# A macaron transformer block on one core: the head of the first feed-forward with a fixed order on four engines, and a last matrix whose sums begin as products

## The chip, the cores and the metric

One Trainium2 chip, of which the kernel uses one core. A core has a matrix engine (TensorE, PE in the profile), a vector engine (VectorE, DVE), a scalar engine (ScalarE, ACT), a general engine (GpSimd, POOL) and an engine that mostly issues transfers (SyncE, SP). Matrix products are accumulated in PSUM, eight banks of 512 fp32 columns; everything else lies in SBUF or DRAM. The metric is the device time of one execution in microseconds (us), the median of the runs.

## The reference

One block of a streaming encoder works on a stream `h` of 16 meta tokens and 1024 frames, 1040 tokens of width 1024, in fp32:

```python
h = h + 0.5 * swiglu(rmsnorm(h, ffn1_norm[l]), ffn1_w_gate[l], ffn1_w_up[l], ffn1_w_down[l])
u = rmsnorm(h, mix_norm[l])
...
h = h + mixed @ w_out[l]
h = h + 0.5 * swiglu(rmsnorm(h, ffn2_norm[l]), ffn2_w_gate[l], ffn2_w_up[l], ffn2_w_down[l])
return rmsnorm(h, final_norm)[:, N_META:]
```

`swiglu(x, g, u, d)` is `(silu(x @ g) * (x @ u)) @ d` with an inner width of 2816. In the middle stand sliding-window attention and gated linear attention; the change leaves them alone.

## The kernel before, in words

**Numbers in two parts.** Each fp32 operand of a product is cut into a high part of the type fp32r, rounded by a copy on ACT, and a low part, the difference, taken on DVE. A product is then three matmuls: high by high, high by low, low by high. Cuts of weights are `plain_cut` (L272 to L282: ACT cast L278, subtraction L279), cuts of operands are `halves` (L288: ACT L291, DVE L292).

**Feed-forward in blocks of seven products.** The inner width is 22 blocks of 128. The last two (f = 20, 21: "heads") and the first two are computed as plain products in the head of the kernel; the other 18 use one level of Strassen's method: two halves of the tokens (520 each in the first feed-forward) by two halves of the width, seven products in place of eight (`PRODUCTS`), with sums of operands (`token_sums`, lines L309 to L315) and of weights (`Group.sums`, L492). All big products are issued at L508.

**The head of the first feed-forward.** Tokens stand in four chunks q0 to q3 of 256 or 264 tokens (`CH`, L569). SP loads rows of x and the weights of the head blocks. `put(q, m)` transposes a tile of x on TensorE (L597, tile `xps`), scales it and cuts it. For q0 and q1 (`first_put`, L607 to L611) the token's root mean square is not known yet: products run on the unscaled operand and `empty` multiplies the result by the root afterwards (L682). For q2 and q3 (`second_put`) ACT copies the raw tile (L622, `xr`), DVE makes the scaled operand (L623, `ub`), ACT casts the high part (L624) and DVE subtracts for the low part (L625). `head_products` (matmuls L672 to L674, PSUM tiles `pg` and `pu`, one bank each) makes gate and up of one head block on one chunk and runs "hooks", other work put between its 16 groups of three matmuls. `head_out` (L689 to L692) is silu, product and cut of the result. Squares for the roots are `square_x`, the roots are `root` (a POOL copy L645 makes the tile to be turned), their spreading over partitions is `spread`. `rescale(m)` (L631 and `halves`) scales the operand of q0 and q1 in place once the roots are there.

The order of ACT and DVE in this head is written by hand (`manual_schedule`); that of TensorE, SP and POOL is left to a scheduler. The order of blocks is (f, q) = (0,q0), (1,q0), (0,q1) and so on; the pair (q, f) is the key of the table `hooks`. Then `more(0)` and `more(1)` make blocks 0 and 1 on the four chunks from q0 to q3, and `token_sums` prepares the operands of the big products, which begin at 138.55 us.

**The last matrix.** `down` runs 10 steps of 7 slots. A step is one half of a group of four inner blocks; a slot is one Strassen product on two output rows, 24 matmuls. All blocks of h (16 of 128 x 520, or 512 in the second feed-forward) are loaded from DRAM at its start (`load_h`, L405), and after each product `add_half` (L408, DVE) adds half of a PSUM tile to one of them. SP loads the operands `tm` (L414, from DRAM where the gate and up stage put them) and the weights `raw` (L426, four parts of 256 KB a step); later groups' `tm` go through ACT's queue. `pump` writes out ("keeps") what the gate and up stage left over: ACT cast L300, DVE subtraction L301, two writes L302 and L303 on SP, from four buffers (`ttile`). The weights of a step are summed on POOL (L492) and cut by `halves` two slots ahead of their use.

After it, the remaining head blocks are multiplied (L801), the sum is finished (L408) and the operand of the projection is made (L130, L131). The 16 meta tokens are gathered in a small tile, cut (L812, L813), and 16 copies of 128 x 16 on POOL (L815, L816) put the parts into the projection's operands; squares of h (L821) and their sums on DVE (L823) follow for the next norm. The projection's products are L97 to L99.

Of the kernel before, what the change touches and what calls it, by code (L numbers as in the profile page):

```python
# [8 lines left out]
F32 = mybir.dt.float32  # L9
# [26 lines left out]
def hybrid_kernel(  # L36
# [29 lines left out]
    def ttile(name, dt=F32, n=512):  # L66
        return tmp.tile([P, TW], dt, tag="t", name=name)[:, 0:n]
# [168 lines left out]
    class Seven:  # L236
# [162 lines left out]
            self.ending = True  # L399


        def load_h(self, ms, r, c):
            for m in ms:
                self.h[m + r][c] = self.block("h2")
                nc.sync.dma_start(out=self.h[m + r][c], in_=self.h_src[c, m + r])  # L405

        def add_half(self, hm, ps):
            nc.vector.scalar_tensor_tensor(hm, ps, 0.5, hm, op0=ALU.mult, op1=ALU.add)  # L408

# [18 lines left out]
            return Group(self, *raws)  # L428

        def down(self, h_src):  # L430
            self.h, self.h_src = [[None] * 2 for _ in range(KT)], h_src
# [12 lines left out]
            for step in range(2 * NG):  # L444
                kg, half = step // 2, step % 2
                if half == 0:
                    ts, nxt = nxt, {}
                last = step == 2 * NG - 1
                for i, (r, c) in enumerate(WHERE):
                    if i + AHEAD < 7:  # L450
# [5 lines left out]
                    if kg + 1 < NG:  # L456
                        self.load_t(kg + 1, nxt, 7 * half + i, nc.scalar)
                    w = made.pop(0)
                    pss = [group.product(i, w, ts, (j * P, 2 * P + j * P), j, step) for j in range(2)]
# [79 lines left out]
    def load_x(t, eng):  # L539
        eng.dma_start(out=xt[t], in_=x[t * P:(t + 1) * P, :])  # L540
# [75 lines left out]
    def second_put(q, m, ps):  # L616
        c, c0, n = CH[q]
        if c0 == 0:
            ub[1][m], B[1][m] = ffn1.block("ub"), ffn1.operand(False, "tb")
        raw = s_pool.tile([P, WB], F32, tag="s", name="xr")[:, 0:n]  # L620
        u, hi = ub[1][m][:, c0:c0 + n], B[1][m][:, c0:c0 + n]
        nc.scalar.copy(raw, ps)  # L622
        nc.vector.scalar_tensor_tensor(u, ps, vec[:, G1 + m:G1 + m + 1], racc[:, N1 + c0:N1 + c0 + n], op0=ALU.mult, op1=ALU.mult)  # L623
# [60 lines left out]
    def head_out(f, q, pss=None):  # L684
        c, c0, n = CH[q]
        x, a = kept[f, c], ttile("a")[:, 0:n]
        hi, lo = x[:, c0:c0 + n], x[:, N1 + c0:N1 + c0 + n]
        g, u = pss or (hi.bitcast(F32), lo.bitcast(F32))
        nc.scalar.activation(a, g, AF.Silu)  # L689
        nc.vector.tensor_mul(a, u, a)  # L690
        nc.scalar.copy(hi, a)
        nc.vector.tensor_sub(lo, a, hi.bitcast(F32))  # L692
        if c0:
            nc.sync.dma_start(out=ffn1.last_dram[f, c], in_=x.bitcast(F32))

    with tc.manual_schedule(engines={nc.scalar.engine, nc.vector.engine}):
        turn_g1()
        square_x(0)  # L700
        square_x(1, eng=nc.vector)
        heads, done = [[], []], {}
        cuts = []
        for i in range(2):
            w, parts = ffn1.plain_cut(head_raws[i], nc.gpsimd if i else None, False)
            heads[0].append(w)
            cuts.append(parts)

        def cut(f, i, eng=None):
            heads[f].append(ffn1.plain_cut(head_raws[2 * f + i], eng))  # L710

        def put(q, m):
            (first_put if q < 2 else second_put)(q, m, turn_x(q, m))

        def do(fn, *a, **k):
            return lambda: fn(*a, **k)

        def emptied(f, q):
            return lambda: empty(f, q, done.pop((f, q)))

        def out_of(f, q):
            return lambda: head_out(f, q, done.pop((f, q), None))

        for m in range(KT):
            put(0, m)
            if m in (0, 3):
                cuts[0][m // 3]()
                cuts[1][m // 3]()
        v = nc.vector
        hooks = {  # L730
            (0, 0): {0: [do(root, 0)], 2: [do(cut, 1, 0, nc.gpsimd)], 6: [do(spread, 0), do(cut, 1, 1)],
                     9: [do(put, 1, 0)], 12: [do(put, 1, 1)], 14: [do(put, 1, 2)]},
            (0, 1): {0: [do(put, 1, 3)], 2: [do(put, 1, 4)], 4: [do(put, 1, 5)], 6: [do(put, 1, 6)], 8: [do(put, 1, 7)],
                     9: [do(square_x, 2, eng=v), do(square_x, 8, NM)], 11: [emptied(0, 0)], 12: [do(square_x, 3, eng=v)]},
            (1, 0): {0: [do(root, 1)], 1: [emptied(1, 0), do(square_x, 6)], 3: [do(square_x, 4, eng=v)], 5: [do(square_x, 7)],
                     6: [do(square_x, 5, eng=v)], 9: [do(spread, 1)], 11: [do(root, 2), do(root, 3)]},
            (1, 1): {0: [emptied(0, 1)], 3: [do(spread, 2), do(spread, 3)],
                     **{5 + m: [do(put, 2, m)] for m in range(KT)}},
            (2, 0): {2: [emptied(1, 1), out_of(0, 0)], **{4 + m: [do(put, 3, m)] for m in range(KT)}, 12: [out_of(1, 0)]},
            (2, 1): {0: [out_of(0, 1)], 2: [out_of(1, 1)], 4: [out_of(0, 2)],  # L740
                     **{5 + m: [do(rescale, m)] for m in range(KT)}},
            (3, 0): {4: [out_of(1, 2)]},
            (3, 1): {2: [out_of(0, 3)]},
        }
        for q in range(4):
            for f in range(LAST):
                done[f, q] = head_products(q, heads[f], hooks[q, f], f == 0)
# [20 lines left out]

    more(0)
    out_of(1, 3)()  # L770
    more(1)
    ffn1.token_sums(ub, between)
    turn_rest()
# [38 lines left out]
    nc.scalar.copy(mh, mt)  # L812
    nc.vector.tensor_sub(ml, mt, mh.bitcast(F32))  # L813
    for m in range(KT):
        nc.gpsimd.tensor_copy(n2.hi[m][:, S:T], mh[:, m, :])  # L815
        nc.gpsimd.tensor_copy(n2.lo[m][:, S:T], ml[:, m, :])  # L816
    for m in range(KT):
        for c in range(2):
            a = sums1[:, c * N1:(c + 1) * N1]
# [772 lines left out]
```

## Time and profile before

| what | value |
|---|---|
| time, median of 3 runs | 2083.16 us (2080.94 to 2083.75) |
| the profiled execution, its own time | 2081.6 us |
| its span, first to last instruction | 2079.9 us |
| mean granted clock of TensorE | 0.988 |
| TensorE busy | 2035.0 us (98%) |
| VectorE, ScalarE, GpSimd busy | 1354.7 (65%), 817.3 (39%), 205.2 us (10%) |

The profiled execution is one of its own, 1.56 us under the median; 1.7 us of it lie outside the span. Times inside the kernel are counted from the span's start. "L508" is line 508 of the kernel. In the lists, `out<-in` names the tiles an instruction writes and reads; the engine after "<-" is what ended the wait. The granted clock is the share of full speed at which TensorE's clock ran.

### The profile page before, as it was taken

To read this page: it belongs to the slowest core of one execution; us is meant where nothing else is said; L and a number is where in the kernel's file an instruction comes from. 1 tells how busy PE (TensorE), PEld (TensorE's weight loads), DVE (VectorE), ACT (ScalarE), POOL (GpSimd) and SP (SyncE) were. 2 spreads that over 40 slices of the span, in tenths; PEclk is the share of its full clock that TensorE was granted. 3 is DMA by queue.
4 is the path that set the end of the run, shared out by engine and by line. 5 is a ranking of instruction groups with operands and counts; after the bars stand their busy time and mean duration, and the time that the engine had idled before them with its cause. 6 is when DMAs were issued, how large, how long until landed. Compare 5 with 4: busy or idle time off the path is not lost.

```text
span 2079.9 us, 31770 instructions
## 1 busy us (share of the span) xinstructions
PE 2035.0 (98%) x12177; PEld 1805.6 (87%) x12177; DVE 1354.7 (65%) x2303; ACT 817.3 (39%) x1551; POOL 205.2 (10%) x240
## 2 busy tenths in 40 slices
PE   8899999999799999999999999999999999999998
PEld 7799999999799988888897778888888888878888
DVE  5866677667577775775345335567876767758775
ACT  5534444443222254664324222344444544422222
POOL 1000000001222171000100000120000000014212
PEclk9899999999999999999999999999999999999999
DMA  6324344349976131125311225641543543599722
GB/s 200 108 84 150 119 156 170 124 144 353 341 246 240 56 99 50 62 61 155 112 41 58 70 66 158 217 143 51 170 165 131 171 154 131 203 378 351 263 81 82
DMA packets 271657, 317.73 MB, mean 153 GB/s; under 512 B 23943, under 2 KB 187905, under 8 KB 271505
## 3 DMA queue, kind: packets, MB, share of 16 engines
q1 hardware_dynamic: 253856, 254.30, 37.2%
q10 hardware_dynamic: 17296, 61.29, 7.8%
q8 instruction: 96, 1.57, 0.3%
q14 instruction: 57, 0.46, 0.1%
q0 software_dynamic: 352, 0.11, 0.1%
HBM read 208.01 MB, written 107.63 MB: 152 GB/s over the span
## 4 chain that ended last, share of the span: by engine, by line
PE 90%; DMA 4%; DVE 3%; ACT 1%; issue 1%; POOL 1%; SPq 0%; DVEq 0%; POOLq 0%; ACTq 0%
PE pb L508 30%; PE pd L508 15%; PE pa L508 8%; PE pj L97 6%; PE pj L98 6%; PE pj L99 6%; PE br L97 1%; PE br L99 1%; PE br L98 1%; PE wo L97 1%; PE wo L98 1%; PE wo L99 1%; PE pd L801 1%; DMA tm<-f2mid 1%; PE tp L1057 1%; DMA h<-h_dram 1%
## 5 line engine op out<-in xcount | busy, mean ns | idle before, releaser
L508 PE MATMUL pb<-tt,wop 128*128 128x260 f32 (+1 forms) x2016 | 337.2, 321 | 0.0
L508 PEld LDWEIGHTS pb<-tt,wop 128*128 128x128 f32 x2016 | 294.5, 188 | 28.1
L508 PE MATMUL pb<-tm,wop 128*128 128x260 f32 (+1 forms) x1440 | 240.8, 323 | 15.9 <-DVE h L408 9.5
L291 ACT CAST wop<-s 128x512 fp32r<-128x512 f32 x232 | 143.7, 622 | 263.7 <-PE pb L508 90.5
L508 PEld LDWEIGHTS pb<-tm,wop 128*128 128x128 f32 x1440 | 211.6, 192 | 37.5 <-DVE h L408 8.7
L97 PE MATMUL pj<-u2h,whi 128*128 128x512 f32 (+2 forms) x608 | 230.3, 379 | 3.1 <-DVE o L1311 1.7
L98 PE MATMUL pj<-u2l,whi 128*128 128x512 f32 (+2 forms) x608 | 225.1, 370 | 3.3 <-POOL u2l L816 3.3
L99 PE MATMUL pj<-u2h,wlo 128*128 128x512 f32 (+2 forms) x608 | 225.2, 370 | 0.0
L292 DVE TENSOR_TENSOR wop<-s,wop 128x512 fp32r<-128x512 f32 x232 | 167.6, 724 | 86.4 <-ACT wop L291 85.9
L291 ACT CAST wop<-raw 128x512 fp32r<-128x512 f32 x174 | 108.3, 623 | 237.9 <-PE pb L508 112.5
L408 DVE SCALAR_TENSOR_TENSOR h<-pb,h 128x520 f32<-128x520 f32 (+1 forms) x160 | 110.4, 694 | 62.0 <-PE pb L508 59.5
L492 POOL TENSOR_TENSOR s<-raw 128x512 f32<-128x512 f32 x28 | 38.7, 1383 | 1087.5 <-DMA raw<-in_ffn_w_down 498.1
L97 PEld LDWEIGHTS pj<-u2h,whi 128*128 128x128 f32 x608 | 115.3, 190 | 22.6 <-issue 2.2
L98 PEld LDWEIGHTS pj<-u2l,whi 128*128 128x128 f32 x608 | 115.4, 190 | 18.7 <-POOL u2l L816 3.5
L99 PEld LDWEIGHTS pj<-u2h,wlo 128*128 128x128 f32 x608 | 115.1, 189 | 17.2
L292 DVE TENSOR_TENSOR wop<-raw,wop 128x512 fp32r<-128x512 f32 x174 | 122.1, 703 | 6.7 <-ACT wop L291 6.5
L508 PE MATMUL pd<-tm,wop 128*128 128x260 f32 (+1 forms) x720 | 118.9, 318 | 1.9 <-DVE h L408 1.8
L508 PEld LDWEIGHTS pd<-tm,wop 128*128 128x128 f32 x720 | 103.8, 188 | 12.0 <-DVE h L408 1.5
L192 ACT CAST whi<-raw 128x1024 fp32r<-128x1024 f32 x58 | 60.8, 1048 | 134.5 <-PE pj L98 77.5
L508 PE MATMUL pb<-tb,wop 128*128 128x260 f32 (+1 forms) x672 | 112.4, 321 | 1.1 <-DVE m L762 1.1
L508 PE MATMUL pa<-tb,wop 128*128 128x260 f32 (+1 forms) x672 | 112.3, 320 | 0.0
L508 PE MATMUL pd<-tb,wop 128*128 128x260 f32 (+1 forms) x672 | 112.3, 320 | 0.0
(379 smaller groups left out, 3771.5 us busy)
## 6 DMA issues: line engine op xcount, KB each, us to landing
tm<-f1mid ACTq DMA_DIRECT2D x56, 520.0 KB, 5.9
tm<-f2mid ACTq DMA_DIRECT2D x56, 512.0 KB, 5.9
raw<-in_ffn_w_gate SPq DMA_DIRECT2D x43, 512.0 KB, 3.9
raw<-in_ffn_w_up SPq DMA_DIRECT2D x43, 512.0 KB, 4.0
raw<-in_ffn_w_down SPq DMA_DIRECT2D x80, 256.0 KB, 6.2
f1mid<-kh SPq DMA_DIRECT2D x70, 260.0 KB, 2.8
f1mid<-kl SPq DMA_DIRECT2D x70, 260.0 KB, 2.7
f2mid<-kh SPq DMA_DIRECT2D x70, 256.0 KB, 2.9
```

The lines of the kernel that those rows point to most:

```text
L97: nc.tensor.matmul(ps, wh[k], xh[k], start=(k == 0), stop=False)
L98: nc.tensor.matmul(ps, wh[k], xl[k], start=False, stop=False)
L99: nc.tensor.matmul(ps, wl[k], xh[k], start=False, stop=(k == n - 1))
L192: nc.scalar.copy(hi[:, 0:cols], raw[:, 0:cols])
L291: nc.scalar.copy(x[:, 0:n], src)
L292: nc.vector.tensor_sub(x[:, n:2 * n], src, x[:, 0:n].bitcast(F32))
L408: nc.vector.scalar_tensor_tensor(hm, ps, 0.5, hm, op0=ALU.mult, op1=ALU.add)
L492: (eng.tensor_add if add else eng.tensor_sub)(a[s], a[x], a[y])
L508: nc.tensor.matmul(ps, y, x[:, c0 + s0:c0 + s0 + sn], start=(first and k == 0 and at == 0), stop=(at == 2 and k == len(cols) - 1), skip_gr ...
L801: nc.tensor.matmul(ps, y, x[:, c0 + s0:c0 + s0 + sn], start=(n == 0), stop=(n == 3 * LAST - 1), skip_group_check=True)
L1057: nc.tensor.transpose(ps[0:k, ga * P:(ga + 1) * P], s.p[:, ga, off:off + k], ident)
```

## The change

It has four parts.

1. **Head.** SP and TensorE get a written order as well (`manual_schedule` over four engines). The weights of the first head block come in four parts of four k-tiles, mixed with the loads of x. All sixteen transposes of q0 stand ahead on TensorE. Squares, roots, cuts and puts sit at other hooks; POOL's cut of a second head weight has no POOL copy ahead of it, the first head block's low parts are all subtracted on DVE, and the puts of q2 come three hooks later. The last subtraction of `second_put` and the second half of `head_out` are returned as a function and run behind the next put or output (`later`).
2. **Order of chunks.** `more` goes through q2, q3, q0, q1.
3. **Last matrix** (both feed-forwards). No h is loaded at the start. The first product of each of the 16 blocks is written as half of the PSUM tile by ACT. The old h comes later: two blocks a step in steps 1 to 8, through a `ttile` buffer, and DVE adds each a step after its load. Operands of the next group are loaded four slots later, and `pump` runs at slots 0, 1, 2, 4, 5, 7 and 8.
4. **Small copies.** The 16 copies of the meta tokens go from POOL to ACT.

On TensorE, at the start of `more(0)`; names with buffer numbers, `tb_185` an operand of q0 after its rescale, `tb_577` and `tb_591` operands of q2. Before:

```order
L672 MATMUL pg_1013<-tb_185,whi_1003 128x256
L672 MATMUL pu_1014<-tb_185,whi_1009 128x256
L673 MATMUL pg_1013<-tb_185,whi_1003 128x256
L674 MATMUL pg_1013<-tb_185,wlo_1004 128x256
L673 MATMUL pu_1014<-tb_185,whi_1009 128x256
L674 MATMUL pu_1014<-tb_185,wlo_1010 128x256
```
After:

```order
L690 MATMUL pg_1015<-tb_577,whi_1005 128x256
L691 MATMUL pg_1015<-tb_577,whi_1005 128x256
L692 MATMUL pg_1015<-tb_577,wlo_1006 128x256
L690 MATMUL pg_1015<-tb_591,whi_1005 128x256
L691 MATMUL pg_1015<-tb_591,whi_1005 128x256
L692 MATMUL pg_1015<-tb_591,wlo_1006 128x256
```
The chunk that stands first is q2, whose operands are made by the puts, where it was q0.

On DVE, the last two rescales and the first output that follows (of head block 1 on q2, the 128x256 product). Before:

```order
L631 SCALAR_TENSOR_TENSOR ub<-ub,vec,racc 128x520
L311 TENSOR_TENSOR ub<-ub 128x520
L309 TENSOR_TENSOR ub<-ub 128x520
L292 TENSOR_TENSOR tb<-ub,tb 128x520
L631 SCALAR_TENSOR_TENSOR ub<-ub,vec,racc 128x520
L310 TENSOR_TENSOR ub<-ub 128x520
L315 TENSOR_TENSOR ub<-ub 128x520
L292 TENSOR_TENSOR tb<-ub,tb 128x520
L690 TENSOR_TENSOR a<-pu,a 128x256
```
After (L649 is `rescale`, L708 and L712 are `head_out`):

```order
L649 SCALAR_TENSOR_TENSOR ub<-ub,vec,racc 128x520
L311 TENSOR_TENSOR ub<-ub 128x520
L309 TENSOR_TENSOR ub<-ub 128x520
L292 TENSOR_TENSOR tb<-ub,tb 128x520
L649 SCALAR_TENSOR_TENSOR ub<-ub,vec,racc 128x520
L310 TENSOR_TENSOR ub<-ub 128x520
L309 TENSOR_TENSOR ub<-ub 128x520
L292 TENSOR_TENSOR tb<-ub,tb 128x520
L708 TENSOR_TENSOR a<-pu,a 128x256
```
The product of the output still stands behind the eighth rescale; only the pairing of the token sums (L309 to L315) differs.

On SP, at the start of the first feed-forward's last matrix (`h` blocks loaded, `tm` operands, kept pairs `kh` and `kl`, `raw` weights). Before:

```order
L405 DMA h_5920<-x_dram 128x520
L414 DMA tm<-f1mid 128x1040 x2
L302 DMA f1mid<-kh 128x520
L303 DMA f1mid<-kl 128x520
L405 DMA h_5980<-x_dram 128x520
L405 DMA h_5982<-x_dram 128x520
L302 DMA f1mid<-kh 128x520
L303 DMA f1mid<-kl 128x520
L405 DMA h_6024<-x_dram 128x520
L405 DMA h_6026<-x_dram 128x520
L426 DMA raw_6233<-in_ffn_w_down 128x2x256 x2
L426 DMA raw_6236<-in_ffn_w_down 128x2x256
```
After:

```order
L409 DMA tm<-f1mid 128x1040 x10
L302 DMA f1mid<-kh 128x520
L303 DMA f1mid<-kl 128x520
L302 DMA f1mid<-kh 128x520
L303 DMA f1mid<-kl 128x520
L421 DMA raw_6191<-in_ffn_w_down 128x2x256 x2
L421 DMA raw_6194<-in_ffn_w_down 128x2x256 x2
L302 DMA f1mid<-kh 128x520
L303 DMA f1mid<-kl 128x520
L302 DMA f1mid<-kh 128x520
```
The loads of h are gone from between the operands and the kept pairs, and the third step's weights (`raw`, L421) stand behind the second kept pair, where the last part of them stood behind the seventh.

The diff, cut to its core:

```diff
-            nxt, AHEAD = {}, 2
+            AHEAD, LATE = 2, 4
...
-                self.load_t(0, nxt, at, nc.sync)
-                if at == 1:
-                    self.load_h((0, 1), 0, 0)
+                self.load_t(0, ts[0], at, nc.sync)
...
-                if at in (5, 7, 11):
-                    self.load_h((0, 1), *{5: (0, 1), 7: (4, 1), 11: (4, 0)}[at])
...
-                        self.add_half(self.by_parts(self.h[2 * half + j + r][c]), pss[j])
-                    self.pump()
-                    if step == 0 and i < 4:
-                        self.load_h((2, 3), *((0, 0), (0, 1), (4, 1), (4, 0))[i])
+                        m = 2 * half + j + r
+                        if self.h[m][c] is None:
+                            self.h[m][c] = self.block("h2")
+                            nc.scalar.activation(self.by_parts(self.h[m][c]), pss[j], AF.Copy, scale=0.5)
+                        else:
+                            self.add_half(self.by_parts(self.h[m][c]), pss[j])
+                    if slot in (0, 1, 2, 4, 5, 7, 8):
+                        self.pump()
+                    if step and i in (1, 4):
+                        if step > 1:
+                            m, c, x = coming.pop(0)
+                            nc.vector.tensor_add(self.h[m][c], self.h[m][c], x)
+                        if old and not last:
+                            m, c = old.pop(0)
+                            x = ttile("old", n=self.n)
+                            nc.sync.dma_start(out=x, in_=h_src[c, m])
+                            coming.append((m, c, x))
...
+    head_raw(0, 0)
     load_x(1, nc.sync)
-    head_raws = [ffn1.plain_raw(cols_view(w, HEADS[0] * P)) for w in (ffn1_w_gate, ffn1_w_up)]
+    for i, k in ((1, 0), (0, 4), (1, 4)):
+        head_raw(i, k)
...
-        nc.vector.tensor_sub(B[1][m][:, N1 + c0:N1 + c0 + n], u, hi.bitcast(F32))
         nc.sync.dma_start(out=x_dram[1, m, :, c0:c0 + n], in_=raw)
+        return lambda: nc.vector.tensor_sub(B[1][m][:, N1 + c0:N1 + c0 + n], u, hi.bitcast(F32))
...
-            (0, 0): {0: [do(root, 0)], 2: [do(cut, 1, 0, nc.gpsimd)], 6: [do(spread, 0), do(cut, 1, 1)],
-                     9: [do(put, 1, 0)], 12: [do(put, 1, 1)], 14: [do(put, 1, 2)]},
+        (0, 0): {6: [cut(1, 0, nc.gpsimd)], 8: [do(square_x, 1, eng=v)], 10: [cut(1, 1)], 12: [put(1, 0)], 14: [put(1, 1)]},
...
-                     **{5 + m: [do(put, 2, m)] for m in range(KT)}},
+                 **{8 + m: [put(2, m)] for m in range(KT)}},
...
-                     **{5 + m: [do(rescale, m)] for m in range(KT)}},
-            (3, 0): {4: [out_of(1, 2)]},
-            (3, 1): {2: [out_of(0, 3)]},
+                 **{8 + m: [do(rescale, m)] for m in range(KT)}},
+        (3, 0): {4: [out_of(1, 2)], 5: [later]},
+        (3, 1): {4: [out_of(0, 3)], 5: [later]},
...
-        for q, (c, c0, n) in enumerate(CH):
+        for q in (2, 3, 0, 1):
+            c, c0, n = CH[q]
...
-        nc.gpsimd.tensor_copy(n2.hi[m][:, S:T], mh[:, m, :])
-        nc.gpsimd.tensor_copy(n2.lo[m][:, S:T], ml[:, m, :])
+        nc.scalar.copy(n2.hi[m][:, S:T], mh[:, m, :])
+        nc.scalar.copy(n2.lo[m][:, S:T], ml[:, m, :])
```

More of the change, by code (lines that the diff above doesn't have):

```diff
@@ L399, in gate_ups @@
             self.ending = True
[L402 to L405, printed above, removed]
         def add_half(self, hm, ps):
@@ L430, in down @@
         def down(self, h_src):
[L431 to L432 removed]
+            self.h = [[None] * 2 for _ in range(KT)]
+            AHEAD, LATE = 2, 4
+            ts, old, coming = [{} for _ in range(NG)], [(m, c) for m in range(KT) for c in range(2)], []
             group = self.load_weights(0)
             for at in range(14):
[L435 to L437 removed]
+                self.load_t(0, ts[0], at, nc.sync)
                 if at == 3:
                     follow = self.load_weights(1)
[L440 to L441 removed]
             group.sums(nc.vector)
@@ L444, in down @@
             for step in range(2 * NG):
-                kg, half = step // 2, step % 2
-                if half == 0:
-                    ts, nxt = nxt, {}
+                half = step % 2
                 last = step == 2 * NG - 1
                 for i, (r, c) in enumerate(WHERE):
+                    slot = 7 * step + i
                     if i + AHEAD < 7:
@@ L455, in down @@
                         made.append(follow.weights(i + AHEAD - 7))
-                    if kg + 1 < NG:
-                        self.load_t(kg + 1, nxt, 7 * half + i, nc.scalar)
+                    kg, at = 1 + (slot - LATE) // 14, (slot - LATE) % 14
+                    if 0 < kg < NG:
+                        self.load_t(kg, ts[kg], at, nc.scalar)
                     w = made.pop(0)
-                    pss = [group.product(i, w, ts, (j * P, 2 * P + j * P), j, step) for j in range(2)]
+                    pss = [group.product(i, w, ts[step // 2], (j * P, 2 * P + j * P), j, step) for j in range(2)]
                     for j in range(2):
-                        self.add_half(self.by_parts(self.h[2 * half + j + r][c]), pss[j])
-                    self.pump()
-                    if step == 0 and i < 4:
-                        self.load_h((2, 3), *((0, 0), (0, 1), (4, 1), (4, 0))[i])
+                        m = 2 * half + j + r
[15 more added lines that the diff above has]
+                            coming.append((m, c, x))
                 if not last:
@@ new lines, in rest, with cut @@
+        def rest():
+            nc.scalar.copy(hi, a)
+            nc.vector.tensor_sub(lo, a, hi.bitcast(F32))
+            if c0:
+                nc.sync.dma_start(out=ffn1.last_dram[f, c], in_=x.bitcast(F32))
+        return rest
+    turn_g1()
+    square_x(0)
+    heads, done, behind = [[], []], {}, []
+    v = nc.vector
+    cuts = []
+    for i in range(2):
+        w, parts = ffn1.plain_cut(head_raws[i], None, False)
+        heads[0].append(w)
+        cuts.append(parts)
+    def cut(f, i, eng=None):
+        return lambda: heads[f].append(ffn1.plain_cut(head_raws[2 * f + i], eng))
@@ new lines, in later, with put, go, do @@
+    def later():
+        while behind:
+            behind.pop(0)()
+    def put(q, m):
+        def go():
+            ps = turn_x(q, m)
+            if q < 2:
+                first_put(q, m, ps)
+            else:
+                rest = second_put(q, m, ps)
+                later()
+                behind.append(rest)
+        return go
+    def do(fn, *a, **k):
+        return lambda: fn(*a, **k)
+    def emptied(f, q):
+        return lambda: empty(f, q, done.pop((f, q)))
+    def out_of(f, q):
+        def go():
+            rest = head_out(f, q, done.pop((f, q), None))
+            later()
+            behind.append(rest)
+        return go
@@ new lines, in hybrid_kernel @@
+    turned = [turn_x(0, m) for m in range(KT)]
+    for m in range(KT):
+        first_put(0, m, turned[m])
+        if m in (0, 3):
+            cuts[0][m // 3]()
+            cuts[1][m // 3]()
+    hooks = {
+        (0, 0): {6: [cut(1, 0, nc.gpsimd)], 8: [do(square_x, 1, eng=v)], 10: [cut(1, 1)], 12: [put(1, 0)], 14: [put(1, 1)]},
+        (0, 1): {0: [do(root, 0), put(1, 2)], 2: [put(1, 3)], 4: [put(1, 4)], 6: [put(1, 5)], 8: [put(1, 6)], 10: [put(1, 7)],
+                 12: [do(spread, 0)], 13: [do(square_x, 8, NM), do(square_x, 2, eng=v)]},
+        (1, 0): {0: [emptied(0, 0)], 1: [do(square_x, 6)], 2: [do(square_x, 3, eng=v)], 4: [emptied(1, 0)],
+                 5: [do(square_x, 7)], 6: [do(square_x, 4, eng=v)], 9: [do(root, 1)], 10: [do(square_x, 5, eng=v)],
+                 13: [do(root, 2), do(root, 3)]},
+        (1, 1): {0: [do(spread, 1)], 1: [emptied(0, 1)], 7: [do(spread, 2), do(spread, 3)],
+                 **{8 + m: [put(2, m)] for m in range(KT)}},
+        (2, 0): {2: [emptied(1, 1)], 3: [out_of(0, 0)], **{4 + m: [put(3, m)] for m in range(KT)}, 13: [out_of(1, 0)]},
+        (2, 1): {0: [out_of(0, 1)], 2: [out_of(1, 1)], 4: [out_of(0, 2)], 6: [later],
+                 **{8 + m: [do(rescale, m)] for m in range(KT)}},
+        (3, 0): {4: [out_of(1, 2)], 5: [later]},
+        (3, 1): {4: [out_of(0, 3)], 5: [later]},
+    }
@@ L748, in hybrid_kernel @@
+    for q in range(4):
+        for f in range(LAST):
+            done[f, q] = head_products(q, heads[f], hooks[q, f], f == 0)
+    manual.__exit__(None, None, None)
     ffn1.tops.update(B11=B[0][0:4], B21=B[0][4:8], B12=B[1][0:4], B22=B[1][4:8])
@@ L770, in hybrid_kernel @@
     out_of(1, 3)()
+    later()
     more(1)
```

51 lines of the change are left out of this document (8 added, 43 removed).

## The prediction, made before the result

> **What bounds the kernel now.** I read the page first, then the list of what TensorE waited for, then the chain of waits in the stretches that list points to, then busy time by stretch. The page says whose time it is:
>
> ```profile
> PE 2035.0 (98%) x12177; PEld 1805.6 (87%) x12177; DVE 1354.7 (65%) x2303; ACT 817.3 (39%) x1551; POOL 205.2 (10%) x240
> ```
>
> TensorE is the bound, so an edit can only give back time that TensorE loses, idle or at a low granted clock. The waits over the whole span (waiting matmul and line, what it waited for, us in total, times, longest):
>
> ```profile
> PE pb L508 <- DVE h L408: 9.5, 2, 8.5
> PE pb L508 <- DMA tm<-f2mid: 4.6, 4, 2.6
> PE pg L673 <- DVE tb L292: 2.9, 6, 0.8
> PE pj L98 <- POOL u2l L816: 3.3, 1, 3.3
> ...
> PE pb L508 <- DMA tm<-f1mid: 1.8, 2, 1.5
> ...
> PE pj L97 <- DVE h L408: 1.2, 1, 1.2
> ```
>
> The stretches they lie in, each row with its length, the busy time and count of each engine, the granted clock (PEclk), the DMA share and rate:
>
> ```profile
> 0.00:24.00 24.00, 17.29 (x83) 13.91 (x83) 7.87 (x20) 10.56 (x23) 6.84 (x16) 0.86 1.00 302
> ...
> 76.00:100.00 24.00, 18.75 (x85) 15.11 (x84) 23.14 (x38) 10.60 (x21) 0.00 (x0) 0.64 0.27 80
> 100.00:139.00 39.00, 37.88 (x317) 37.66 (x316) 19.40 (x36) 13.26 (x28) 0.00 (x0) 1.00 0.10 36
> ...
> 518.00:532.00 14.00, 12.18 (x87) 11.79 (x86) 8.35 (x13) 2.30 (x4) 0.00 (x0) 0.88 1.03 392
> 532.00:549.00 17.00, 14.10 (x114) 13.53 (x113) 8.77 (x14) 3.44 (x6) 0.00 (x0) 1.00 1.02 369
> 549.00:563.00 14.00, 5.53 (x34) 5.33 (x33) 7.47 (x9) 2.99 (x5) 10.77 (x8) 0.76 0.82 270
> ...
> 740.00:764.00 24.00, 19.39 (x121) 18.65 (x120) 16.06 (x31) 10.20 (x17) 18.55 (x42) 0.93 0.36 89
> ...
> 1852.00:1868.00 16.00, 12.09 (x41) 9.12 (x40) 4.82 (x8) 1.86 (x3) 0.00 (x0) 0.79 1.02 390
> 1868.00:1900.00 32.00, 32.00 (x142) 26.47 (x142) 25.05 (x38) 7.37 (x12) 12.67 (x9) 1.00 1.01 363
> ```
>
> At full clock a matmul of about 260 columns takes 37.88/317 = 0.1195 us (row 100 to 139), one of 512 takes 32.00/142 = 0.225 us (row 1868 to 1900). Length less count times that is what a stretch loses: 0 to 24 us 24 - 83 x 0.1195 = 14; 76 to 100 us 13.8 (its clock of 0.64 alone is 8.6 of it); 518 to 563 us 3.6 + 3.4 + 9.9 = 16.9; 1852 to 1868 us 16 - 41 x 0.225 = 6.8. In 740 to 764 us, where shapes are mixed, idle time 24 - 19.39 = 4.6 and clock 24 x 0.07 = 1.7 make 6.3. That is 58 us within the change's reach.
>
> **The head, to 139 us.** A "quarter" is the 48 matmuls of one f-block on one of the four token chunks q0 to q3, 48 x 0.1195 = 5.74 us. Rows of the chain before 100 us (start, length, what), then two timeline rows:
>
> ```profile
> 43.37 0.50 DVE ub L623
> ...
> 44.76 0.41 DVE ub L623
> ...
> 59.53 0.39 PE pg L672
> ...
> 75.32 4.77 DMA raw<-in_ffn_w_up
> ...
> 81.25 1.23 DVE wlo L279
> ...
> 88.09 0.67 DVE ub L631
> 88.76 0.61 DVE ub L311
> ...
> 89.98 0.61 DVE tb L292
> ...
> 93.80 0.63 ACT tb L291
> ```
>
> ```profile
> 23.68 2.37 POOL L279 TENSOR_TENSOR wlo<-rawx,whi 128x1024 fp32r<-128x1024 f32 x1
> ```
>
> ```profile
> 73.40 0.76 DVE L631 SCALAR_TENSOR_TENSOR ub<-ub,vec,racc 128x520 f32<-128x520 f32 x1
> ```
>
> Start: the second head block cannot begin before POOL's cut ends, 23.68 + 2.37 = 26.05. The change puts that cut ahead of the spreading copies and makes the transposes first, so the first quarter is paced by the put copies alone. I take the cut's end 3.6 us earlier, and give 0.6 back because the puts of q2 stand three hooks later in the next block (3 x 3 x 0.1195 = 1.1 at most): 3 us, between 0 (POOL's cut slower beside a busier DVE) and 5. The weights in parts move the same bytes; their first product starts a little earlier, inside that range.
>
> POOL's price may move. In 740 to 764 us eight small copies beside DVE's adds of two inputs took 9.76 us, eight after them 1.16:
>
> ```profile
> 746.47 9.76 POOL L815 CAST u2h<-mth 128x16 fp32r<-128x16 f32 x8 [1.88 <-ACT mth L812]
> ...
> 756.27 1.16 POOL L816 CAST u2l<-mtl 128x16 fp32r<-128x16 f32 x8
> ```
>
> [...] A cut of 5 us in place of 2.37 would cost the start about its whole gain, which is the range's 0.
>
> The delayed subtraction of the second puts (43.37 to 44.76: 1.3 us a put) I cost at nothing either way. Today a put is DVE product, ACT cast, DVE subtraction. Afterwards the next product still waits for ACT's next raw copy, which stands behind the cast on ACT: same length.
>
> The rescales: DVE begins them at 73.40 now. They come 3 us earlier with the rest, 1.2 because a weight cut (81.25: 1.23) goes behind the first of them, and by estimate 2.5 because the outputs (L690, L692) overlap in pairs: 66.7.
>
> The new chunk order: before, q0 runs first and each of its products follows its rescale. Afterwards q2 and q3, which need none. The second quarters (2,1), (3,0), (3,1) run from 59.53 to 59.53 + 3 x 5.74 = 76.8 now, 73.8 afterwards, and q2 ends at 79.5. But q3 needs two of the eight PSUM banks, and all eight are taken: the pair that comes free is that of (1,2), emptied by its silu on ACT, which stands behind the eighth rescale's cast. DVE's rows to there: 8 x 0.67 rescales, 7 x 0.61 subtractions L292, 7 x 0.61 token sums, 4 x 1.23 cuts make 18.8, and about 0.9 waiting for the second weights (4.77 us from issue to landing): 66.7 + 19.7 = 86.4. ACT's 0.63 cast and the silu, 0.4 by estimate, end at 87.4. So the waits of q0 go, and q3 waits 87.4 - 79.5 = 8 us instead. After such a stall the clock is half for a few us: 549 to 563 us has 0.76, 14 x 0.24 = 3.4 us of it partly under the stall; I take 1.9. Then seven quarters as now from 98 us, where the chain of rescales ends, to 138.55: 40.5. The big products start at 87.4 + 1.9 + 40.5 = 129.8, not 138.55: **8.7 us**, from 4 (start term 0) to 14 (rescales earlier still).
>
> **The last matrix of the first feed-forward, 500 to 563 us.** The chain there:
>
> ```profile
> 508.13 12.88 DMA tm<-f1mid
> ...
> 542.42 9.42 DMA raw<-in_ffn_w_down
> ...
> 552.03 1.23 POOL s L492
> ...
> 554.63 0.63 ACT wop L291
> ...
> 558.70 2.97 PE pb L508 x12
> ```
>
> A transfer takes 12.88 us with DMA share 1.03: the queue is full. The 16 loads of h are 260 KB each (16 x 0.266 = 4.3 MB, 10.9 us at 392 GB/s). They stand on SP among the tm loads and then among the kept tiles' writes, so the third step's last weights leave only at 542.42 and land at 551.84; POOL's sums, ACT's cast and a DVE operation ahead of L408 follow, and TensorE waits 8.5. Afterwards no h is loaded there; those weights stand after the second kept pair, and pumps are spread over slots 0 to 8. The weights then leave before 524 us by the order, 18 us earlier, and 9.42 later is still before need. What is late next is ACT, which waits in order for a buffer of the kept tiles at slots 6 to 8: 1 to 2 us and perhaps a clock step. The trace shows that a short wait can cost that: 518 to 532 us waited 1.8 us in all, and its clock is 0.88, 14 x 0.12 = 1.7 us.
>
> [...]
>
> Costs added, by rows of the page and of the groups of ACT:
>
> ```profile
> L408 DVE SCALAR_TENSOR_TENSOR h<-pb,h 128x520 f32<-128x520 f32 (+1 forms) x160 | 110.4, 694 | 62.0 <-PE pb L508 59.5
> ```
>
> ```profile
> L379 ACT COPY u<-pd 128x520 f32<-128x520 f32 x18 | 10.7, 595 | 23.7 <-PE pd L508 23.7
> ```
>
> Sixteen ACT copies (16 x 0.6 = 9.5 us) replace sixteen DVE additions in steps 0 and 1; sixteen DVE additions of about 0.69 us come in steps 2 to 9, two in each of 20 us, with DVE 65% busy: under TensorE, nothing. Without that cover they would cost 11 us. The next tm loads leave four slots later:
>
> ```profile
> tm<-f1mid ACTq DMA_DIRECT2D x56, 520.0 KB, 5.9
> ```
>
> The last then has 3 slots of 24 matmuls (3 x 2.87 = 8.6 us) against 5.9 us to land, so it stays hidden by 2.7 us. I leave 2.9 of 16.9: **14 us**, from 7 to 16.9.
>
> **The sixteen small copies after it.** They go from POOL to ACT; ACT's nearest row:
>
> ```profile
> 763.04 0.40 ACT L146 ACTIVATE u2t<-tot,eps_t 128x8 f32<-128x8 f32 x2 [11.07 <-PE tot L137]
> ```
>
> 16 x 0.2 = 3.2 us from 746.5 end before 750, where POOL's first eight now last to 746.47 + 9.76 = 756.2. The 3.3 and 0.2 waits and the 1.7 of clock go; the squares behind the copies on ACT shift by 3.2 but DVE's sums of them have until the totals. The 1.2 wait for L408 stays. 6.3 - 1.2 - 0.4 = **4.7 us**, from 3 to 5.2.
>
> **The second feed-forward's last matrix.** Its chain before the loss:
>
> ```profile
> 1832.02 9.20 DMA h<-h_dram
> ...
> 1847.84 12.39 DMA tm<-f2mid
> ```
>
> The first eight h loads (8 x 0.262 MB at 390 GB/s = 5.4 us) leave the queue ahead of that tm, which is up to 6 us late. Of 6.8 I take **6 us**, from 3 to 6.8.
>
> **Sum.** 8.7 + 14 + 4.7 + 6 = 33.4. The profiled execution was 2081.6 us (span 2079.9 and 1.7 around it), 1.56 under the median of 2083.16: 2081.6 - 33.4 = 2048.2, as a median 2049.8.
>
> **Rivals.**
> *The bank wait does not bind.* If the silu of (1,2) were free early, q3 would follow q2 and the 8 + 1.9 us stay with us: 2040. Against: eight banks, and the emptying stands behind the casts.
> *The last matrices give half.* Kept pairs' writes and the ACT copies hold ACT's casts of weights in steps 0 and 1 (7 casts of 0.63, copies and kept casts fill some 14 of 20 us): 10 of 20 us kept, 2060; with the start at 0 also, 2064.
> *Slower: the loads of old h hold the weights.* They go through four buffers shared with the kept pairs and stand on SP ahead of a step's weights; an old h waits for DVE's addition of the one four before. If that held each step's weights past their need, all eight steps in both matrices pay. It decides at 33.4/16 = 2.1 us a step; at 3 us a step the result is 2083.2 + 48 - 33.4 = 2098. Against: old h is added one step after its load, so two of four buffers are in use.
> *No effect.* The losses come back in other places (q3, ACT): 2083, within the 0.2% (4 us) that a measurement here can tell.
>
> **How the numbers follow.** The forecast 0.62, the bank rival 0.08, half 0.20, no effect 0.04, slower 0.06. Low: the bank rival, 2039; high: half with no start gain and the copies' lower bound, 2066. Faster 0.90, same 0.04, slower 0.06.
>
> **What would show it.** Right: a TensorE wait of about 8 us for ACT's silu near 79 us and none for L292; big products starting near 130 us; no wait over 2 us between 500 and 563; none for POOL at 752; no h load on SP before step 1. Wrong: q3 without a wait; weights leaving SP after 530 us; TensorE waiting for old h or for weights of steps 3 to 9.

## The result, and the profile after

The changed kernel takes 2053.1 us (2051.31 to 2056.41, 4 runs) where the kernel before takes 2083.45: a ratio of 0.9855, 95% interval 0.9835 to 0.9876, or 30 us, for 33.4 forecast. In a later set of runs the same kernel took 2054.28 (ratio 0.9862, 0.9849 to 0.9876). The two profiled executions took 2056.41 (span 2054.7) and 2052.64 us (span 2050.9). The page of the first, and its waits over the whole span (waiting matmul, what it waited for, us in total, times, longest):

```profile
PE 2024.0 (99%) x12177; PEld 1801.9 (88%) x12177; DVE 1359.7 (66%) x2305; ACT 835.0 (41%) x1599; POOL 195.2 (10%) x222
```

```profile
PE pg L690 <- ACT a L707: 6.4, 1, 6.4
PE pb L515 <- DVE h L403: 3.6, 1, 3.6
PE pb L515 <- ACT h L458: 3.5, 2, 2.1
PE xps L613 <- DVE ub L641: 2.1, 5, 0.7
PE pj L97 <- DVE o L1350: 1.7, 1, 1.7
PE xps L615 <- DMA x<-in_x: 1.5, 1, 1.5
PE pg L692 <- POOL wlo L279: 1.3, 1, 1.3
...
PE pj L97 <- DVE h L403: 1.2, 1, 1.2
```

Of the six old waits that the prediction lists five are gone: VectorE in the weights' chain (9.5), the operands of both last matrices, the rescales, POOL's copies. The 1.2 for L403 (L408 before) stayed, as forecast. New are the wait for the silu of the PSUM pair (6.4; forecast 8) and waits for the first sums on ACT and for VectorE's additions (L403) in the last matrices.

TensorE executes the same 12,177 matmuls in both kernels, the big products and all behind them in the same order, so the start of matmul number n can be compared from trace to trace. The lead over the kernel before, from the first matmul on, in us:

| stretch | forecast | first profile | second profile |
|---|---|---|---|
| head, to the first big product | 8.7 | 6.1 | 6.5 |
| gate and up stage | 0 | -0.5 | -0.5 |
| first last matrix | 14 | 9.1 | 10.6 |
| small copies, projection | 4.7 | 5.5 | 5.5 |
| middle of the kernel | 0 | 0.1 | 1.8 |
| second last matrix, rest | 6 | 4.7 | 4.9 |
| sum | 33.4 | 25.1 | 28.8 |

Nothing was changed in the middle of the kernel. Its row shows how a profiled execution can mislead by 1.7 us; the section on the hardware comes back to it. The second profile is the better one to compare with the medians.

The first profile by stretches (length, busy time and count of each engine, granted clock, DMA share and rate), where before had 0.64, 0.88 and 0.76:

```profile
500.00:515.00 15.00, 13.61 (x112) 13.22 (x111) 8.10 (x14) 5.02 (x9) 0.00 (x0) 1.00 0.97 358
515.00:530.00 15.00, 11.43 (x73) 11.21 (x72) 7.96 (x11) 6.04 (x12) 5.11 (x4) 0.77 0.98 342
```

```profile
79.00:94.00 15.00, 8.64 (x56) 8.44 (x55) 15.00 (x27) 7.49 (x16) 0.00 (x0) 0.77 0.26 78
```

Two things to see: the loss of the first last matrix now lies in one stretch of 30 us that loses 30 - (112 + 73) x 0.1195 = 7.9 us, with the DMA queue still full (share 0.97 and 0.98); and VectorE is busy for every one of the 15 us around TensorE's wait in the head.

### The profile page after: what moved, and what is told of

It reads as the page before. It is cut to its first block, busy times and chain, and to the rows that moved or that the text cites. A ratio compares the mean times of both kernels' runs of the same rounds, so it can differ in the third digit from the quotient of the medians.

```text
span 2054.7 us, 31806 instructions
## 1 busy us (share of the span) xinstructions
PE 2024.0 (99%) x12177; PEld 1801.9 (88%) x12177; DVE 1359.7 (66%) x2305; ACT 835.0 (41%) x1599; POOL 195.2 (10%) x222
## 4 chain that ended last, share of the span: by engine, by line
PE 92%; DMA 4%; DVE 2%; ACT 1%; issue 1%; SPq 0%; DVEq 0%; POOLq 0%; ACTq 0%
PE pb L515 30%; PE pd L515 15%; PE pa L515 7%; PE pj L97 6%; PE pj L98 6%; PE pj L99 6%; PE br L97 1%; PE br L99 1%; PE br L98 1%; PE wo L97 1%; PE wo L98 1%; PE wo L99 1%; PE pd L840 1%; DMA tm<-f2mid 1%; PE tp L1096 1%; DMA f1mid<-kl 1%
## 5 line engine op out<-in xcount | busy, mean ns | idle before, releaser
L403 DVE SCALAR_TENSOR_TENSOR h<-pb,h 128x520 f32<-128x520 f32 (+1 forms) x136 | 93.8, 693 | 41.6 <-PE pb L515 39.4
```

## The experiments

All times are medians beside runs of the kernel before on the same chip. That kernel took 2080.74 to 2084.0 us in the four sets of runs, so kernels of different sets are compared by their ratios to it; 0.001 is 2.1 us, and a difference of two ratios is uncertain by some 0.002, or 4 us. Eight traces of the study have the changed head as it stands. In them the first rescale starts at 66.61 to 69.03 us and the first big product at 130.53 to 134.45 us; a single trace of another head is to be measured by this scatter.

### The order of the chunks alone

```diff
-        for q in (2, 3, 0, 1):
+        for q in (0, 1, 2, 3):
```

> The changed kernel with the first two blocks' chunks back in the order q0 to q3. Theory (the head's end is set by VectorE's eight rescales, which now begin about 6 us earlier, and the new order only trades the wait for them against a wait for a PSUM pair that is emptied behind them): within 2 us of the changed kernel's 2053, big products starting at 131 to 134 us. Rival (the order of the chunks is what the head gained): about 6 us slower, 2059, big products at 138.

Measured 2054.33 us, ratio 0.9869 (0.9854 to 0.9883), the changed kernel within its interval; the first big product starts at 130.98 us, inside the scatter of the changed head (132.44 in the first profile). Its waits between 60 and 140 us:

```profile
PE pg L690 <- ACT tb L291: 1.7, 3, 0.6
PE pg L691 <- DVE tb L292: 1.6, 3, 0.6
PE pb L515 <- DVE m L800: 1.1, 1, 1.1
```

The wait for the pair is gone and the waits for rescaled operands are back: as VectorE's chain stands, the new order brings nothing. What the head won fits VectorE's rescales beginning earlier, 67.38 us in the changed kernel where they began at 73.40: that is 6.0 of the 6.1 to 6.5.

### Outputs ahead of the rescales

```diff
-        (2, 1): {0: [out_of(0, 1)], 2: [out_of(1, 1)], 4: [out_of(0, 2)], 6: [later],
-                 **{8 + m: [do(rescale, m)] for m in range(KT)}},
-        (3, 0): {4: [out_of(1, 2)], 5: [later]},
-        (3, 1): {4: [out_of(0, 3)], 5: [later]},
+        (2, 1): {0: [out_of(0, 1)], 2: [out_of(1, 1)], 4: [out_of(0, 2)], 6: [later]},
+        (3, 0): {0: [out_of(1, 2)], 1: [later], **{8 + m: [do(rescale, m)] for m in range(4)}},
+        (3, 1): {4: [out_of(0, 3)], 5: [later], **{8 + m: [do(rescale, 4 + m)] for m in range(4)}},
```

> The changed kernel with the output of (1,q2) ahead of all rescales and that of (0,q3) between the fourth and the fifth. Theory (the wait of 6.4 us near 82 us is for a PSUM pair that is emptied behind the rescales): that wait goes, q3 follows q2, the first rescaled chunk is needed only near 85 us, and big products start 7 to 10 us earlier, about 2044. Rival (VectorE's chain sets the end in any order): the wait only moves to the rescaled chunk, gain under 3 us, 2050 to 2053.

Measured 2045.45 us, ratio 0.9828 (0.9813 to 0.9842), 0.0027 to 0.0034 under the changed kernel's two ratios, or 6 to 7 us. Its waits between 60 and 130 us, in place of the 6.4:

```profile
PE pg L691 <- DVE tb L292: 0.7, 1, 0.7
PE pb L515 <- ACT vec L88: 0.5, 1, 0.5
```

The first big product starts at 123.62, 8.4 us (matched matmul by matmul) ahead of the changed kernel's second profile. With the pair emptied in time the kernel wins what the new order did not win alone. Outputs ahead of the rescales in the old order were not run, so it is not shown that this edit needs the new order.

### TensorE's order left to the scheduler

```diff
-    manual = tc.manual_schedule(engines={nc.scalar.engine, nc.vector.engine, nc.tensor.engine, nc.sync.engine})
+    manual = tc.manual_schedule(engines={nc.scalar.engine, nc.vector.engine, nc.sync.engine})
```

> The changed kernel with TensorE's order in the head left to the scheduler again, SP, ACT and DVE written. TensorE was 5 us ahead of the kernel before at 23 us and level with it at 59 us. Theory (VectorE's chain decides the end, TensorE's lost lead costs nothing): within 2 us of 2053. Rival (TensorE's written order, which puts matmuls behind transposes that wait for a bank, loses the lead): 3 to 5 us faster, 2048 to 2050.

Measured 2051.29 us, ratio 0.9856 (0.9841 to 0.9871). The time alone tells nothing, since the difference is smaller than the interval. The trace does: the first second put on VectorE, the first rescale (L649) and the first big product come at 39.72, 65.39 and 129.09 us, where the changed kernel's second profile has them at 41.48, 67.15 and 132.03. The first rescale in this kernel, then in the changed one (second profile):

```profile
65.39 0.75 DVE L649 SCALAR_TENSOR_TENSOR ub<-ub,vec,racc 128x520 f32<-128x520 f32 x1
```

```profile
67.15 0.75 DVE L649 SCALAR_TENSOR_TENSOR ub<-ub,vec,racc 128x520 f32<-128x520 f32 x1
```

Rescale and big product lie 1.2 and 1.4 us before the earliest of the eight traces. So my theory falls in part: VectorE's chain does decide, but it hangs on TensorE's transposes, and their written place costs it 1 to 3 us by these traces. The rival's number was too large.

### The small copies back on POOL

```diff
-        nc.scalar.copy(n2.hi[m][:, S:T], mh[:, m, :])
-        nc.scalar.copy(n2.lo[m][:, S:T], ml[:, m, :])
+        nc.gpsimd.tensor_copy(n2.hi[m][:, S:T], mh[:, m, :])
+        nc.gpsimd.tensor_copy(n2.lo[m][:, S:T], ml[:, m, :])
```

> The changed kernel with the 16 small copies back on POOL. Theory (POOL's copies beside VectorE's additions of two inputs are what the projection waits for): 4.5 to 6 us slower, 2058 to 2059, with TensorE waiting over 3 us for the copies again. Rival (ACT's copies only shifted the wait to the squares and totals): within 2 us of 2053.

Measured 2058.88 us, ratio 0.9889 (0.9872 to 0.9905): 0.0027 to 0.0034 or 6 to 7 us over the changed kernel, and the old wait is back to the tenth:

```profile
PE pj L98 <- POOL u2l L855: 3.3, 1, 3.3
```

From the last matrix to the end of the projection this trace is 6.5 us longer than the changed kernel's second, and level with it everywhere else within 0.3 us.

### The old last matrix

`down` and `load_h` as before, all else changed.

```diff
-                        if self.h[m][c] is None:
-                            self.h[m][c] = self.block("h2")
-                            nc.scalar.activation(self.by_parts(self.h[m][c]), pss[j], AF.Copy, scale=0.5)
...
+                        self.add_half(self.by_parts(self.h[2 * half + j + r][c]), pss[j])
+                    self.pump()
+                    if step == 0 and i < 4:
+                        self.load_h((2, 3), *((0, 0), (0, 1), (4, 1), (4, 0))[i])
```

> The changed kernel with the last matrix of both feed-forwards as before (h loaded at the start, all sums added on VectorE, pumps in every slot of the first step). Theory (the two profiled executions, matched matmul by matmul, show 9 us won in the first and 5 in the second): 12 to 16 us slower than the changed kernel, 2065 to 2069. Rival (the prediction's 14 + 6): 20 us, 2073.

Measured 2071.34 us, ratio 0.9950 (0.9937 to 0.9962): 0.0088 or 18 us over the changed kernel (ratio of its second set of runs), nearer to the prediction's 20 than to the 14 that I had read from one pair of profiles. Matched with the second profile the traces give 12.0 and 4.7, 16.7 in all; 1.6 more lies in the middle, where nothing differs, so some of the 18 is chance. Its waits are those of before:

```profile
PE pb L508 <- DVE h L408: 9.6, 1, 9.6
...
PE pb L508 <- DMA tm<-f2mid: 3.7, 4, 2.5
```

### Kept pairs spread wider

```diff
-                    if slot in (0, 1, 2, 4, 5, 7, 8):
+                    if slot in (0, 2, 5, 8, 11, 14, 17):
```

> The changed kernel with the kept pairs written out at slots 0, 2, 5, 8, 11, 14 and 17 instead of 0 to 8. Theory (the waits of 3.6 and 1.4 us left in the first last matrix, and the half clock after them, come from ACT and VectorE standing at the pairs' four buffers while the queue is full): 5 to 9 us faster, 2044 to 2048, no wait over 1 us between 505 and 525 us. Rival (the queue is simply full, and pairs later meet the loads of old h and the next weights): 2050 to 2056, with waits further on.

Measured 2051.92 us, ratio 0.9862 (0.9848 to 0.9875): no gain. One wait went and another came, for ACT's first sum again:

```profile
PE pa L515 <- ACT h L458: 3.8, 1, 3.8
PE xps L615 <- DMA x<-in_x: 2.3, 1, 2.3
PE pb L515 <- ACT h L458: 2.1, 1, 2.1
```

Spreading the pairs wins nothing; that theory falls. It does not clear the buffers, though: in this trace too ACT's cast for a pair, ahead of the sum that TensorE waits 3.8 us for, stands 5.16 us until the write of an older pair has landed (516.6 to 521.75 us).

### First sums on VectorE

```diff
-                            nc.scalar.activation(self.by_parts(self.h[m][c]), pss[j], AF.Copy, scale=0.5)
+                            nc.vector.tensor_scalar(self.by_parts(self.h[m][c]), pss[j], 0.5, None, op0=ALU.mult)
```

> The changed kernel with the 16 first sums written by VectorE in place of ACT. Theory (both engines stand at the same four buffers, so it does not matter which one writes): within 2 us of 2053. Rival (the copies on ACT behind the pairs' casts are what TensorE waits for): 2 to 5 us faster, 2048 to 2051. Third (VectorE has no room left in the first two steps): 2 to 4 us slower.

Measured 2061.25 us, ratio 0.9896 (0.9881 to 0.9911), 0.0034 or 7 us over the changed kernel; the third reading of the expectation, and beyond its number. TensorE waits longer for VectorE, 5.0 of it before 530 us:

```profile
PE pb L515 <- DVE h L403: 7.8, 2, 5.0
```

The copies are therefore not free on VectorE, and ACT is the better one of the two.

### Operands four slots earlier

```diff
-            AHEAD, LATE = 2, 4
+            AHEAD, LATE = 2, 0
```

> The changed kernel with the next group's operands loaded four slots earlier, as before. Theory (they join a full queue in the first step and delay the pairs): 1 to 5 us slower, 2054 to 2058, with longer waits between 505 and 525 us. Rival (the queue's order, not its load, decides): within 1 us of 2053.

Measured 2050.35 us, ratio 0.9850 (0.9837 to 0.9864), no slower: the four slots bring nothing that can be measured, and the theory that these loads fill the queue finds no support.

### The changed kernel again

> The changed kernel itself, beside the others of this call. All clock changes of the traces lie on one grid of 3.41 us, so the same wait may or may not be followed by a half clock, by where it falls. Theory: the median is 2050 to 2054, and a second profile shows the same waits of over 1 us as the first (6.4 for ACT's silu, 3.6 and 1.4 in the first last matrix, 1.7 near 1101 us) with half-clock stretches at other places. Rival (the first profile's waits were a chance of that execution): waits of another size or place.

Measured 2054.28 us (2052.64 to 2059.3), ratio 0.9862. The waits over the whole span stand in the same places and, but for the first loads of x (L615: 1.5, now 2.6), each within half a us (one of the two for ACT's first sums now stands under `pa`, with 1.0):

```profile
PE pg L690 <- ACT a L707: 6.2, 1, 6.2
PE pb L515 <- DVE h L403: 3.4, 1, 3.4
PE xps L615 <- DMA x<-in_x: 2.6, 1, 2.6
...
PE pb L515 <- ACT h L458: 1.9, 1, 1.9
PE pj L97 <- DVE o L1350: 1.7, 1, 1.7
```

The half clock came at other places only in part. Both profiles have some from 24 to 60 us (granted clock 0.93 in the first, 0.95 in the second) and in the first 24 us (0.96 and 0.93); near 1104 us the first alone has it (0.88 over 14 us, 1.00 in the second). Over the whole span the clock is 0.992 and 0.994.

### The next group's operands loaded by SP

```diff
-                        self.load_t(kg, ts[kg], at, nc.scalar)
+                        self.load_t(kg, ts[kg], at, nc.sync if kg == 1 else nc.scalar)
```

> The changed kernel with the loads of the second group's operands issued by SP in place of ACT. Theory (the first sum on ACT near 508 us stands behind the issue of such a load, which waits for an older transfer): no wait for ACT's first sums before 512 us, 1 to 4 us faster in all. Rival (the queue is full, and what leaves ACT's way holds SP): the third step's weights, now behind three more pairs and these loads, land after need, 3 to 10 us slower.

Measured 2043.77 us, ratio 0.9812 (0.9799 to 0.9825): 10.5 us under the changed kernel of the same set of runs, more than the theory's 4. Matched with that kernel's profile the trace wins 5.1 us in the first last matrix and 3.9 in the second; in the head and the middle, where nothing was changed, 1.0 comes and 1.5 goes. The reason to try it was this place in the changed kernel's trace, ACT from 502 us (ACTq is ACT's queue issuing a transfer):

```profile
502.71 0.61 ACT L458 ACTIVATE h<-pb 128x520 f32<-128x520 f32 x1 [0.77 <-PE pb L515]
508.75 0.33 ACTq L409 DMA_DIRECT2D tm<-f1mid  x1
509.18 0.60 ACT L458 ACTIVATE h<-pb 128x520 f32<-128x520 f32 x1 [5.87 <-DMA f1mid<-kh]
```

ACT does nothing for six us: its next instruction is the issue of a load, which waits for an older transfer (it leaves 0.02 us after an operand load that SP had issued at 496.64 us has landed, at 508.73), and the first sum behind it is done when TensorE has long finished the product. The same stretches without those issues:

```profile
500.00:515.00 15.00, 15.00 (x127) 15.00 (x127) 10.94 (x17) 9.09 (x17) 0.00 (x0) 1.00 0.79 273
515.00:530.00 15.00, 15.00 (x127) 15.00 (x127) 8.85 (x10) 6.82 (x12) 5.87 (x4) 1.00 0.99 362
```

127 matmuls where there were 112 and 73, and full clock. ACT is 9.09 us busy in the first where it was 5.02. The weights behind the loads on SP (510 to 513 us) still land in time. The edit also thins the queue (273 GB/s for 358), so how much is ACT set free and how much a shorter queue isn't separated; the 5.87 us above, and that loading earlier cost nothing and spreading the pairs won nothing, speak for ACT.

### Outputs first, and TensorE left to the scheduler

Both edits of above.

> The changed kernel with the outputs ahead of the rescales (as in the run with the outputs first) and TensorE's order in the head left to the scheduler. Theory (without the wait for the pair the rescales decide, and TensorE's own order costs nothing): within 1.5 us of the run with the outputs first, 2043 to 2047. Rival (the two gains add up): 2 us or more below it, 2040 to 2043.

Measured 2042.41 us, ratio 0.9806 (0.9792 to 0.9819), 0.0022 or 4.6 us under the kernel with the outputs first: the rival by its number. The trace shows less: matched with the kernel with the outputs first it wins 2.6 us in the head, where the first big product starts at 121.00, and 3.0 in the last matrices, where nothing differs. The next run has the same head and starts its big products at 123.10, 0.5 before the kernel with the outputs first. So what TensorE's written order costs here, 0.5 to 2.6 us, isn't clear of the scatter.

### All three

> The changed kernel with the outputs ahead of the rescales, TensorE's order in the head left to the scheduler, and the second group's operands loaded by SP. Theory (the head's wait and ACT's held sums lie in different stretches, so what they cost adds): 12 + 10 us under the changed kernel's 2054 of the last call, 2030 to 2035. Rival (an earlier head meets the same full queue later, so only the larger of the two is won): 2040 to 2044.

Measured 2035.57 us, ratio 0.9776 (0.9762 to 0.9790): 0.0086 or 18 us under the changed kernel, of 22 if all added, by far nearer to the sum than to the larger part. It is the best version of the study. What waits remain in it are short; its four longest:

```profile
PE xps L615 <- DMA x<-in_x: 2.6, 1, 2.6
PE pj L97 <- DVE o L1349: 1.7, 1, 1.7
PE xps L613 <- DMA x<-in_meta_tokens: 1.3, 1, 1.3
PE warm L560 <- DVE some L555: 1.2, 1, 1.2
```

## Why the prediction was right, and where its terms were off

**What bounds it** was right: all that was won is time that TensorE had lost, and every stretch of the list gave some. The sum was helped a little: without the middle of the kernel the stretches give 25.0 and 27.0 us in the two profiles, of 33.4, where the medians differ by 30; no term of the prediction explains the rest.

**The head, 8.7 forecast, 6.1 to 6.5 measured.** The mechanism was right to the place: q3 waits for ACT's silu of (1,q2) behind the eighth rescale, 6.4 us where 8 were forecast (TensorE came there at 82.8 us instead of 79.5, the silu's end 1.7 us later). The chain in the first profile of the changed kernel, VectorE's first and last rescale, ACT's cast and silu, TensorE's first matmul of q3:

```profile
67.38 0.75 DVE L649 SCALAR_TENSOR_TENSOR ub<-ub,vec,racc 128x520 f32<-128x520 f32 x1
...
87.40 0.75 DVE L649 SCALAR_TENSOR_TENSOR ub<-ub,vec,racc 128x520 f32<-128x520 f32 x1
```

```profile
88.18 0.62 ACT L291 CAST tb<-ub 128x520 fp32r<-128x520 f32 x1 [1.88 <-DVE ub L649]
88.72 0.38 ACT L707 ACTIVATE a<-pg 128x256 f32<-128x256 f32 x1
```

```profile
89.14 0.59 PE L690 MATMUL pg<-tb,whi 128*128 128x264 f32 x1 [6.36 <-ACT a L707]
```

Forecast were 66.7 for the first, 87.4 for the silu's end, 129.8 for the big products; they came at 67.38, 89.1 and 132.44. In all eight traces with this head the big products come 4.1 to 8.0 us earlier than before, less than 8.7 in every one. Two sizes were off. "Start: 3 us" gave 1.7: the second puts began at 41.72 for 43.37. POOL's cut took 2.84 us instead of 2.37, and TensorE waited 1.3 us for it, but it ended at 21.14 for 26.05, and TensorE led by 5 us at 23 us, counted in matmuls. It was level with the kernel before at 59.5 us. Between lie the 2.1 us for L641, where in the order now written transposes that wait for a bank hold the products behind them, and a half clock at 56 us (0.50 for 3.41 us), 1.7 more. And VectorE waited 2.0 us among the rescales, 1.3 of it for ACT's casts of weights and 0.7 for that of an operand, where I had 0.9. What I missed is what the chunk order is worth: I set the earlier rescales and the new order down as one gain. The run with the old order shows that none of it is the order; the rescales' 6.0 us account for it.

**The delayed subtraction at nothing** held: a second put takes 1.23 us (41.72 to 49.09 in six) for 1.3.

**The first last matrix, 14 forecast, 9 to 12 measured** (9.1 and 10.6 from the profiles, 12.0 against the old matrix with the new head). The stall at the weights is gone, as forecast. The remainder was put at 2.9 and is 7.9 in the first profile: 1.39 and 3.57 us of waits and the half clock (0.50 from 520.37 to 527.20 us). What I named as late next, ACT at the kept pairs' buffers, is there, and VectorE stands there too, but each for over 4 us where I had 1 to 2. Ahead of the wait of 3.57 us, on ACT, VectorE and TensorE:

```profile
518.13 0.62 ACT L300 CAST kh<-u 128x520 fp32r<-128x520 f32 x1 [4.62 <-DMA f1mid<-kh]
```

```profile
519.74 0.70 DVE L301 TENSOR_TENSOR kl<-u,kh 128x520 fp32r<-128x520 f32 x1 [4.21 <-DMA f1mid<-kl]
520.36 0.69 DVE L403 SCALAR_TENSOR_TENSOR h<-pd,h 128x520 f32<-128x520 f32 x1
```

```profile
521.11 1.24 PE L515 MATMUL pb<-tm,wop 128*128 128x260 f32 x4 [3.57 <-DVE h L403]
```

What I had not named comes before it: the transfers which ACT itself issues between the copies. The one at 508.75 us, in the rows of the run with the loads on SP, holds ACT for 5.87 us; the wait of 1.39 us is for the sum right behind it, and the pairs' casts come behind that. With the loads on SP ACT's casts of the pairs wait for no buffer from 503 to 513 us, VectorE's subtractions 0.6 us at most, and both waits are gone. That the held issue also makes the longer wait fits this, but the same edit thinned the queue. The term that failed is the sixteen ACT copies at nothing: their 9.5 us do fit, but they inherit the waits of whatever stands ahead of them in ACT's queue. The later loads of four slots, costed at nothing, were nothing.

**The small copies, 4.7 forecast, 5.5 to 6.5 measured.** ACT makes the sixteen from 731.78 to 733.56 us, 0.11 us each where I took 0.2; the whole of the wait and of the clock loss went (granted clock 1.00 from 712 to 740 us).

**The second last matrix, 6 forecast, 4.7 to 4.9 measured.** At 1841 us TensorE waits 2.1 us for a first sum, behind loads' issues on ACT as in the first, and the clock is 0.50 from 1844.74 to 1848.15 us; the run with the loads on SP has no wait there.

**The rivals.** The bank wait did bind. "Half" came nearest of them: of the 20 us of the last matrices 14 to 17 came, where it had 10. No list of the changed kernel has a wait for old h or for weights in the last matrices. The median lies 3 us above the forecast and inside the range.

## What to carry to other kernels

An edit that puts work ahead of a wait pays only when the next resource, here two PSUM banks, is free by then: find what empties it, and move that first. Here the issue of one load from ACT's queue held ACT's own work for 5.87 us, until an older transfer had landed (with such loads taken off ACT the kernel won 10.5 us, a thinner queue included); when sums move to an engine, look at what it issues. When a chain of one engine sets the end of a stage, look for what starts that chain, not for what fills the other engines.

## What the runs showed of the hardware

**The clock changes on a grid.** The stretches of half clock in the first profile of the changed kernel begin at 22.02, 56.15, 86.87, 520.37, 1104.05 and 1844.74 us, and one at 2049.54 runs into the end of the span: all are whole multiples of 3.4133 us apart (56.15 - 22.02 is 10 of them, 1104.05 - 22.02 is 317), and each before the last lasts one or two of them:

```profile
22.02:25.43 3.41, 3.41 (x16) 3.14 (x16) 2.59 (x9) 1.23 (x3) 0.40 (x1) 0.50 1.16 318
56.15:59.56 3.41, 3.41 (x17) 3.41 (x17) 2.19 (x6) 1.73 (x6) 0.00 (x0) 0.50 0.35 114
86.87:93.70 6.83, 4.55 (x20) 4.56 (x21) 6.83 (x14) 4.26 (x12) 0.00 (x0) 0.50 0.00 0
...
1104.05:1107.46 3.41, 3.41 (x10) 2.63 (x9) 3.41 (x6) 3.38 (x7) 1.59 (x1) 0.50 0.03 7
```

In the profile of the kernel before, half clock begins at 9.09, 80.77, 521.09, 555.22, 756.61, 1125.25, 1859.11 and 2077.56 us, again whole multiples of 3.4133 us apart (521.09 - 9.09 is 150 of them).

In the changed kernel's first profile TensorE was without a matmul for 1.27, 1.30, 3.41, 2.84, 1.87, 2.06 and 0.43 us of the 3.41 us ahead of the seven stretches, and in the kernel before for 1.82 us ahead of the one at 521.09. So one of the eight followed 3.41 us that were idle throughout. What sets the grid, and what decides whether a half clock follows a wait, isn't shown.

**The same wait can cost more or less.** Near 1101 us (1122 in the kernel before) every trace has the same wait of 1.7 us for one VectorE instruction, L1350 in the changed kernel. In the kernel before a half clock follows it (granted 0.89 from 1115 to 1128 us). The first profile of the changed kernel has one, the second none:

```profile
1098.00:1112.00 14.00, 12.13 (x57) 8.95 (x55) 10.53 (x18) 8.57 (x17) 2.87 (x2) 0.88 0.25 77
```

```profile
1094.40:1108.40 14.00, 12.12 (x64) 9.16 (x62) 12.17 (x18) 10.17 (x19) 4.52 (x2) 1.00 0.16 54
```

It is the 1.7 us of the table's middle row. That such differences make up the few us between runs of one kernel fits, but wasn't tested.
